# Three idle engines read elements of x into registers at the start of an Lp-pooling kernel

## The chip, the cores and the metric

The kernel runs on one core of one Trainium2 chip. The metric is the device time of one execution in microseconds (us); the time given for a kernel is the median over several runs.

## What is computed

The input x is 32 x 256 x 4096 in float32, p is 2 and the window is 4. For each window of four neighbouring elements the kernel gives the root of the mean of the squares:

```python
for i in range(out_length):
    window = np.abs(x[:, :, 4 * i:4 * i + 4]) ** 2.0
    result[:, :, i] = np.mean(window, axis=-1) ** 0.5
```

The output is 32 x 256 x 1024 in float32. So 134.22 MB are read and 33.55 MB are written.

## The kernel before

**Tiling.** x is taken as one flat line of elements, since windows never cross a row. The line is cut into six blocks (`blocks`, line 51) of four, four, four, four, three and one tiles. Inside a block each of the 128 partitions holds one contiguous stretch (`rows`, line 64). A tile is 128 x 13184 elements (`W`, line 41), a few are narrower, and there are 20 of them. A row of a full tile, 52,736 bytes, is what one packet of a DMA moves; 128 rows over 16 DMA engines make eight packets on each engine. Neighbouring partitions of block 0 lie 52,704 elements apart in x, about 211 KB.

**Buffers.** x has three buffers (`x_tiles`, `X_SLOTS` is 3), so tile i uses buffer i mod 3. The results of a block of four tiles gather in `o_tile` (four places) until the block is stored; a sum that can't go there yet waits in PSUM (`s_tile`).

**Work on one tile.** ScalarE squares the tile in place (`square`, line 89). VectorE adds the first half of each window to the second (`pairs`, line 95), then the two sums that are left (`fours`, line 99). ScalarE takes the root (`root`, line 102). For the last two tiles VectorE squares a part itself (line 155).

**Order of the work.** It is written out by hand (`manual_schedule`): each engine runs its instructions in the order of the text. SyncE issues all loads (line 83): the first three at the very start (the loop over `X_SLOTS`, lines 122 and 123), load i+3 when VectorE is done with tile i. ScalarE issues the stores of the first three blocks from its own queue (line 86), SyncE those of the last three. The loads and SyncE's stores go by queue q1, ScalarE's stores by queue q10; both run on the same 16 DMA engines. TensorE has nothing to do in the kernel, GpSimd nothing but four small fills of constants before it. A barrier of all engines stands ahead of the kernel's first instruction (line 189 in the profile) and another after its last (line 203).

Of the kernel before, what the change touches and what calls it, by code (L numbers as in the profile page):

```python
# [1 line left out]

# [4 lines left out]


@with_exitstack
def kernel(  # L10
    ctx: ExitStack,
    tc: tile.TileContext,
    x: bass.AP,
    p: float,
    kernel_size: int,
    out: bass.AP,
):

    nc = tc.nc

    assert float(p) == 2.0, "kernel specialized for p == 2"
    k = int(kernel_size)  # L30
    assert k == 4, "kernel specialized for kernel_size == 4"

    P = nc.NUM_PARTITIONS
    fp32 = mybir.dt.float32
    Act = mybir.ActivationFunctionType
    add = mybir.AluOpType.add
    xf = x.rearrange("b c l -> (b c l)")
    of = out.rearrange("b c l -> (b c l)")
    total = xf.shape[0] // P

    W = 13184
    R = W // k
    X_SLOTS = 3
    NARROW = W - 32
    LAST = total - 18 * W - NARROW
    widths = [W] * 3 + [NARROW] + [W] * 15 + [LAST]
    n = len(widths)
    assert 0 < LAST <= W and LAST % 16 == 0


    blocks = [[0, 1, 2, 3], [4, 5, 6, 7], [8, 9, 10, 11], [12, 13, 14, 15], [18, 16, 17], [19]]
    block_of = {i: b for b, group in enumerate(blocks) for i in group}
    block_width = [sum(widths[i] for i in group) for group in blocks]

    x_pool = ctx.enter_context(tc.tile_pool(name="x_pool", bufs=1))
    o_pool = ctx.enter_context(tc.tile_pool(name="o_pool", bufs=1))
    s_pool = ctx.enter_context(tc.tile_pool(name="s_pool", bufs=1, space=bass.MemoryType.PSUM))
    x_tiles = [x_pool.tile([P, W], fp32, name=f"xt{j}") for j in range(X_SLOTS)]
    o_tile = o_pool.tile([P, 4 * R], fp32, name="ot")
    first = o_pool.tile([P, 1], fp32, name="first")  # L60
    s_tile = s_pool.tile([P, 4096], fp32, name="st")
    ctx.enter_context(tc.manual_schedule())

    def rows(flat, b, div):
        at = sum(block_width[:b]) * P // div
        return flat[at:at + block_width[b] * P // div].rearrange("(p w) -> p w", p=P)


    free = x_tiles[17 % X_SLOTS]
    place = {i: o_tile[:, i % 4 * R:i % 4 * R + widths[i] // k] for i in range(16)}  # L70
    place[18] = free[:, R:2 * R]
    place[19] = free[:, 0:LAST // k]
    place[16] = free[:, 2 * R:3 * R]
    place[17] = free[:, 3 * R:4 * R]
    held = [o_tile[:, 0:w // k] for w in block_width[:4]] + [free[:, R:4 * R], place[19]]

    xs, loads, stores, sums, squares = {}, {}, {}, {}, {}

    def load(i):
        b = block_of[i]  # L80
        at = sum(widths[j] for j in blocks[b][:blocks[b].index(i)])
        xs[i] = x_tiles[i % X_SLOTS][:, 0:widths[i]]
        loads[i] = nc.sync.dma_start(out=xs[i], in_=rows(xf, b, 1)[:, at:at + widths[i]])  # L83

    def store(b, queue):
        stores[b] = queue.dma_start(out=rows(of, b, k), in_=held[b])  # L86

    def square(v):
        return nc.scalar.activation(out=v, in_=v, func=Act.Square)  # L89

    def pairs(v):

        q = v.rearrange("p (n j) -> p n j", j=k)
        h = v[:, 0:v.shape[1] // 2].rearrange("p (n j) -> p n j", j=2)
        return nc.vector.tensor_tensor(out=h, in0=q[:, :, 0:2], in1=q[:, :, 2:4], op=add)  # L95

    def fours(o, v):
        h = v[:, 0:v.shape[1] // 2].rearrange("p (n j) -> p n j", j=2)
        return nc.vector.tensor_tensor(out=o, in0=h[:, :, 0], in1=h[:, :, 1], op=add)  # L99

    def root(o, s):
        return nc.scalar.activation(out=o, in_=s, func=Act.Sqrt, scale=1.0 / k)  # L102

    summed = {i: s_tile[:, 0:R] if i in (4, 8, 12, 16) else place[i] for i in range(n)}

    def roots(*group):
        if len(group) == 1:
            root(place[group[0]], summed[group[0]])
        else:
            v = o_tile[:, group[0] % 4 * R:(group[-1] % 4 + 1) * R]  # L110
            r = root(v, v)
            if group[0] in (5, 9):

                implied(r, stores[block_of[group[0]] - 1])
        if group[-1] in (3, 7, 11):
            store(block_of[group[-1]], nc.scalar)

    def implied(later, earlier):

        tc.declare_no_dep(later.ins, earlier.ins, reason="implied by the other waits")  # L120

    for i in range(X_SLOTS):
        load(i)


    ahead = {4: (3,), 8: (7,), 12: (11,)}
    behind = {3: [(0, 1, 2)], 7: [(5, 6), (4,)], 11: [(9, 10), (8,)], 14: [(12,)], 15: [(13, 14)], 16: [(15,)]}

    root(first[:, :], nc.const_aps.tensor(1.0, (P, 1), fp32))
    for i in range(17):  # L130
        if i in ahead:
            roots(*ahead[i])
        s = square(xs[i])
        squares[i] = s
        if i == 3:
            implied(s, squares[0])
        if i in (3, 7, 11):

            for earlier in sums[i - X_SLOTS]:
                implied(s, earlier)  # L140
        for group in behind.get(i, []):
            roots(*group)
        sums[i] = pairs(xs[i]), fours(summed[i], xs[i])
        if i + X_SLOTS < n:
            load(i + X_SLOTS)

    store(3, nc.sync)
    square(xs[17])
    pairs(xs[17])
    fours(summed[17], xs[17])  # L150
    later = {18: 4608, 19: 2000}

    def shared_square(i):
        v = xs[i][:, 0:later[i]]
        nc.vector.tensor_tensor(out=v, in0=v, in1=v, op=mybir.AluOpType.mult)  # L155
        square(xs[i][:, later[i]:widths[i]])

    def shared_pairs(i):
        implied(pairs(xs[i]), loads[i])

    shared_square(18)
    roots(16)
    roots(17)
    shared_pairs(18)
    fours(summed[18], xs[18])
    shared_square(19)
    roots(18)
    store(4, nc.sync)
    shared_pairs(19)
    fours(summed[19], xs[19])  # L170
    roots(19)
    store(5, nc.sync)


# [1 line left out]
_INS = ['x', 'p', 'kernel_size']  # L176
_OUTS = [((32, 256, 1024), 'float32')]

_NUMBERS = {'p': 2.0, 'kernel_size': 4}


# [26 lines left out]
```

## Time and profile before

| | |
|---|---|
| median of 3 runs | 393.96 us (393.93 to 393.99) |
| span of the profiled execution, first instruction to last | 392.3 us |
| what lies around the span: median less span | 1.7 us |
| HBM read, written | 134.22 MB, 33.55 MB |
| mean rate over the span | 428 GB/s |
| busy: ScalarE (ACT), VectorE (DVE), GpSimd (POOL) | 274.4 us, 218.2 us, 0.2 us |

The profile gives no time of the profiled execution but its span. In the profile's lines SP is SyncE, and a q behind an engine's name (SPq, ACTq, DVEq) stands for its instruction queue: issues and waits, not work. A view of windows cuts the span into stretches that one names; its columns are the stretch, its length, the busy time and the number of instructions of DVE, ACT and POOL, the granted TensorE clock, the DMA share and the rate. It books a DMA packet whole in the stretch in which it starts. So the rate times the length is the size of the packets that started there, and the DMA share times the length times 16, over their number, is how long one of them took.

### The profile page before, as it was taken

The numbers are of one execution on the slowest core, as the hardware profiler recorded it, in microseconds if no ns is written. First come the engines' busy times: TensorE is split into PE (matmuls) and PEld (weight loads), VectorE is DVE, ScalarE is ACT, GpSimd is POOL, SyncE is SP. The second block draws the span as 40 slices with busy tenths as digits, with TensorE's granted clock in tenths as the row PEclk, the third lists the DMA queues.
The fourth block names the chain that finished last, engine by engine and source line by source line (L and its number), as shares of the span: only waits on it lengthen the run. The fifth ranks groups of instructions, "written<-read, shape, count | busy, mean of one in ns | idle before, by whom it ended". The sixth has DMA issues, their size and how long they took to land.

```text
span 392.3 us, 176 instructions
## 1 busy us (share of the span) xinstructions
DVE 218.2 (56%) x42; ACT 274.4 (70%) x37; POOL 0.2 (0%) x4
## 2 busy tenths in 40 slices
DVE  0009477580693274905942748069418485699970
ACT  1095695979950859799509597995098999969910
POOL 0000000000000000000000000000000000000000
DMA  8999999999999999999999999999999999999997
GB/s 344 430 430 430 430 440 435 452 457 366 430 430 430 430 430 430 430 441 446 452 446 441 436 430 436 430 430 430 430 430 430 430 430 430 430 453 415 430 413 342
DMA packets 3744, 167.77 MB, mean 428 GB/s; under 512 B 416, under 2 KB 416, under 8 KB 416
## 3 DMA queue, kind: packets, MB, share of 16 engines
q1 hardware_dynamic: 3312, 147.53, 87.4%
q10 hardware_dynamic: 432, 20.25, 11.9%
HBM read 134.22 MB, written 33.55 MB: 428 GB/s over the span
## 4 chain that ended last, share of the span: by engine, by line
DMA 43%; ACT 30%; DVE 23%; issue 0%; ACTq 0%; SPq 0%; DVEq 0%
DMA xt<-in_x_dram 43%; ACT xt L89 28%; DVE xt L95 14%; DVE ot L99 5%; DVE xt L99 3%; DVE xt L155 2%; ACT ot L102 2%; ACT xt L102 1%; ACTq L86 0%; SPq L83 0%; DVEq L95 0%
## 5 line engine op out<-in xcount | busy, mean ns | idle before, releaser
L89 ACT ACTIVATE xt<-xt 128x13184 f32<-128x13184 f32 (+3 forms) x20 | 216.7, 10847 | 92.3 <-DMA xt<-in_x_dram 91.0
L95 DVE TENSOR_TENSOR xt<-xt 128x6592 f32<-128x6592 f32 (+2 forms) x20 | 139.7, 6985 | 144.1 <-ACT xt L89 143.9
L99 DVE TENSOR_TENSOR ot<-xt 128x3296 f32<-128x3296 f32 (+1 forms) x13 | 46.7, 3592 | 17.9 <-DMA out_dram<-ot 17.6
L102 ACT ACTIVATE ot<-ot 128x6592 f32<-128x6592 f32 (+3 forms) x8 | 37.2, 4655 | 7.0 <-DVE ot L99 7.0
L102 ACT ACTIVATE xt<-xt 128x3296 f32<-128x3296 f32 (+1 forms) x3 | 8.5, 2836 | 8.8 <-DVE xt L99 8.8
L99 DVE TENSOR_TENSOR st<-xt 128x3296 f32<-128x3296 f32 x4 | 14.4, 3600 | 0.1
L99 DVE TENSOR_TENSOR xt<-xt 128x3296 f32<-128x3296 f32 (+1 forms) x3 | 10.4, 3461 | 0.1
L102 ACT ACTIVATE ot<-st 128x3296 f32<-128x3296 f32 x3 | 8.7, 2898 | 0.0
L155 DVE TENSOR_TENSOR xt<-xt 128x4608 f32<-128x4608 f32 (+1 forms) x2 | 7.2, 3593 | 0.0
L102 ACT ACTIVATE xt<-st 128x3296 f32<-128x3296 f32 x1 | 2.9, 2898 | 0.0
L102 ACT ACT_TABLE_LOAD x1 | 1.3, 1283 | 0.7 <-PEq L189 0.7
L102 ACT ACTIVATE first<-const-float32-1.0 128x1 f32<-128x1 f32 x1 | 0.2, 202 | 0.0
L189 POOL MEMSET const-bfloat16-1.0<- 128x1 bf16 x1 | 0.1, 101 | 0.0
L189 POOL MEMSET const-uint8-127<- 128x1 uint8 x1 | 0.1, 101 | 0.0
L189 POOL MEMSET const-float32-0.0<- 128x1 f32 x1 | 0.1, 98 | 0.2 <-issue 0.2
L189 POOL MEMSET const-float32-1.0<- 128x1 f32 x1 | 0.1, 98 | 0.0
## 6 DMA issues: line engine op xcount, KB each, us to landing
xt<-in_x_dram SPq DMA_DIRECT2D x18, 6592.0 KB, 29.8
out_dram<-ot ACTq DMA_DIRECT2D x2, 6592.0 KB, 35.1
out_dram<-ot SPq DMA_DIRECT2D x1, 6592.0 KB, 37.1
out_dram<-ot ACTq DMA_DIRECT2D x1, 6588.0 KB, 36.3
xt<-in_x_dram SPq DMA_DIRECT2D x1, 6576.0 KB, 24.7
xt<-in_x_dram SPq DMA_DIRECT2D x1, 5840.0 KB, 21.9
out_dram<-xt SPq DMA_DIRECT2D x1, 4944.0 KB, 16.1
out_dram<-xt SPq DMA_DIRECT2D x1, 1460.0 KB, 8.2
```

Source lines behind the costliest of these rows:

```text
L89: return nc.scalar.activation(out=v, in_=v, func=Act.Square)
L95: return nc.vector.tensor_tensor(out=h, in0=q[:, :, 0:2], in1=q[:, :, 2:4], op=add)
L99: return nc.vector.tensor_tensor(out=o, in0=h[:, :, 0], in1=h[:, :, 1], op=add)
L102: return nc.scalar.activation(out=o, in_=s, func=Act.Sqrt, scale=1.0 / k)
L155: nc.vector.tensor_tensor(out=v, in0=v, in1=v, op=mybir.AluOpType.mult)
L189: nc = _bacc.Bacc("TRN2", target_bir_lowering=False, num_devices=1)
```

## The change

Ahead of the first three loads, in the text, four reads are added by a loop: each takes the first 32 bits of one partition's stretch of block 0 into a register of an engine. TensorE reads those of partitions 0 and 1, GpSimd that of partition 64, VectorE that of partition 127. Nothing uses the values. No other line is changed.

```diff
+    ints = rows(xf, 0, 1).bitcast(mybir.dt.int32)
+    for engine, p in ((nc.tensor, 0), (nc.tensor, 1), (nc.gpsimd, P // 2), (nc.vector, P - 1)):
+        seen = engine.alloc_register(f"seen{p}")
+        engine.load(seen, ints[p:p + 1, 0:1])
+        engine.keepalive_nop([engine.lower_val_access(seen)])
     for i in range(X_SLOTS):
         load(i)
```

Built, each read of an element is two register loads, one of the address of x (named `in_x_dram_ptr` in the built program) and, after a sum on the register, one of the element. TensorE's program grows from one row, a branch, to seven, with four register loads; GpSimd's and VectorE's get three rows each, two of them register loads. On VectorE they stand ahead of its first addition, on GpSimd behind the four fills and the barrier. The programs of ScalarE and SyncE have the same rows and the same waits as before.

## The prediction

> **What bounds the kernel now.** I read the page first: how busy each engine is, and how full the DMA is.
>
> ```profile
> DVE 218.2 (56%) x42; ACT 274.4 (70%) x37; POOL 0.2 (0%) x4
> ...
> DMA  8999999999999999999999999999999999999997
> ...
> q1 hardware_dynamic: 3312, 147.53, 87.4%
> q10 hardware_dynamic: 432, 20.25, 11.9%
> ```
>
> No engine is full, but the two DMA queues together hold the 16 DMA engines for 87.4% + 11.9% = 99.3% of the span. Only the first and the last slice fall short of nines. The kernel is bound by its transfers, and what can still be won lies at the two ends, or where a packet takes longer than its bytes need.
>
> Next the chain of work that ended last (start, length, what), its first pieces and its last:
>
> ```profile
> 0.66 0.07 issue
> 0.73 18.04 DMA xt<-in_x_dram
> 18.77 0.02 issue
> 18.79 11.20 ACT xt L89
> 29.99 0.02 issue
> 30.01 7.04 DVE xt L95
> ...
> 306.43 24.79 DMA xt<-in_x_dram
> 331.22 0.02 issue
> 331.25 11.20 ACT xt L89
> ...
> 380.49 0.02 issue
> 380.51 2.64 ACT xt L102
> ```
>
> The chain begins with SyncE's first issue at 0.73 and the landing of tile 0 at 18.77. From the landing at 331.22 on it is compute up to 383.15, then the last store. In between, transfers and compute hand over to each other many times, yet the DMA is never out of work: load 3 is issued at 40.75 while load 2 lands only at 49.9. So **the whole program hangs rigidly on the landing of tile 0**: every later issue follows a landing, and every landing follows the packets before it. A microsecond won or lost before 18.77 should be there at the end too, one for one. No row shows a slack that would swallow it.
>
> Last, the windows at the start, and around the first packets of the first and the second store (91.8 and 172.5):
>
> ```profile
> 1.70:2.30 0.60, 0.00 (x0) 0.51 (x2) 0.00 (x0) 1.00 4.24 1318
> 2.30:2.60 0.30, 0.00 (x0) 0.00 (x0) 0.00 (x0) 1.00 0.42 176
> 2.60:4.30 1.70, 0.00 (x0) 0.00 (x0) 0.00 (x0) 1.00 0.00 0
> 4.30:4.85 0.55, 0.00 (x0) 0.00 (x0) 0.00 (x0) 1.00 3.55 1534
> 91.80:92.40 0.60, 0.00 (x0) 0.60 (x1) 0.00 (x0) 1.00 4.82 1406
> 172.50:173.30 0.80, 0.00 (x0) 0.80 (x1) 0.00 (x0) 1.00 2.43 1055
> ```
>
> In the first two, 1318 GB/s x 0.60 us is 15 packets and 176 x 0.30 is one: the first packet of each of the 16 DMA engines. They took (4.24 x 0.60 + 0.42 x 0.30) x 16 / 16 = 2.67 us each. The second packets, from 4.30 on, took 3.55 x 0.55 = 1.95 us, and that stays the pace. So **the first packet costs 0.72 us too much on average**, and no engine starts another before 4.34. By the packet records the first ones start from 1.74 to 2.49 and last 2.01 to 3.00 us, the second ones start from 4.34 to 4.80. Taking 1.95 off, each engine is as if it had begun between 2.39 and 2.85.
>
> The same happens once more. In the window at 91.80, 16 load packets took 4.82 x 0.60 = 2.89 us, 0.94 too much, just as the first store comes on (ScalarE issued it at 90.31). At the second store they took 2.43 x 0.80 = 1.95: nothing.
>
> **The change part by part.** It removes and moves nothing, and adds no wait: the rows of SyncE and ScalarE stay as they are, so no DMA is moved past another.
>
> *The instructions themselves.* TensorE's four register loads, and two each on GpSimd and VectorE, start after the barrier, at about 0.75 us. VectorE's first addition starts at 30.01, because ScalarE's first square ends only then; TensorE and GpSimd have nothing before the barrier at the end, past 391 us. The trace has no register load. The nearest rows are a semaphore instruction on a queue, 0.02 us, from below, and SyncE's issue to its first packet, 0.73 to 1.74, so 1.0 us, from above. Two in a row on VectorE are 0.04 to 2.0 us, beside 29 us of cover; TensorE's four at most 4.0. I take **nothing**. Were the cover gone, VectorE's 2 us would delay the issue of load 3, which has 9 us (40.75 to 49.9) before the queue runs dry.
>
> *What the reads do to the first packets.* This is the only place on the path. Suppose the excess of 0.72 us is paid by whoever first reaches x, and that the three engines' reads can pay it. The element's read leaves after the address is in, at 0.75 plus 0.02 to 1.0, so at 0.77 to 1.75; the DMA's first packet starts at 1.74. The head start is 0 to 0.97 us, the middle 0.48. What it is worth is set by the DMA engine that is last, not by the mean: the last is as if begun at 2.85, and if all excess went, the last would be the one that starts at 2.49 and has hardly any (2.01 against 1.95). So the gain is 2.85 - 2.49 = **0.36 us**; a head start of 0.36 is enough for it, and the middle one gives that. The ends: nothing, and 1.06, if the late starts were part of the excess too and all engines began at about 1.79. Below nothing: reads that stand in front of the DMA's own could cost as much as they can win, 0.36.
>
> [...] No row of before shows a register load.
>
> *Sum.* The profiled execution's 392.3 would become 391.9. The 1.7 us around the span don't change, as no row of them is touched, so the median of 393.96 goes to **393.6**.
>
> **The rivals.**
>
> *The excess isn't about x (393.96).* The window at 91.80 speaks for this: 0.94 us are lost when a second queue starts, on load packets that read x, which had been read for 90 us. At that time no store packet had begun. If the excess is a queue's own start, q1 has one at 1.74 and q10 one at 91.8, and a read from another engine takes away neither. Against it: the first packets of q1 were under way when they lost the time, and `out` is first used at 91.8 as well, so a first touch of a tensor fits both places too; tiles of later blocks, 27 MB on, show no excess.
>
> [...]
>
> *The reads come too late (393.96).* They do what they say, but if a register load takes the full 1.0 us, the element's read leaves at 1.75, with the DMA's own.
>
> *The reads take away more (392.9 to 393.3).* If the staggered starts, 1.74 to 2.49, belong to the excess, the last engine begins at 2.2 (the later spread is 4.34 to 4.80, 0.46) or at 1.79: 0.65 to 1.06 us are won. For it: the last of the 16 starts alone, 0.28 after the one before. Against it: the stagger is mostly what the 0.38 us of SyncE's issue would make.
>
> *Slower (395.0).* If first reaches to x are served one after the other, and two of the three engines' reads go out before 1.74, to stretches of x far apart (partitions 0 and 64, 13.5 MB), the DMA waits for both: 2 x 0.72 us, less the 0.36 that is then paid for it, is 1.08 more. It decides only where the reads are early and take turns. Against it: 16 DMA engines reach 16 places of x at once and lose 0.72 on average, not 16 times that.
>
> **How the numbers follow.** Forecast, 393.6: 0.42. More won: 0.15. Not about x: 0.26. Too late: 0.09. Slower: 0.08. The range, 392.9 to 394.3, takes in the bound of 1.06 and the 0.36 below nothing, and leaves out the slower case and a little. A measurement of this kernel tells about 0.2% (0.79 us) from no change. Over 0.79 won is most of the second case and a little of the first, together 0.15; slower by as much is the last case, 0.08; all else, 0.77, is within.
>
> **What would show it.** Right: the windows from 1.70 to 2.60 give packets of about 2.2 us, tile 0 lands at about 18.4, and the end comes 0.36 earlier. If the packets still take 2.67, the rivals without effect hold. If the first packets start later than 1.74, or take over 2.67, the slower one. The 0.94 at 91.8 should stay. A gain ahead of 18.77 that is not there at the end would refute the rigid chain. If VectorE's first addition starts later than its square's end, the cover was wrong.

## The result, and the profile after

The changed kernel takes **394.45 us** (median of 20 runs, 394.17 to 395.11); the kernel before, beside it, 394.01 us (20 runs, 393.88 to 394.24). The ratio is 1.0012, with a 95% interval of 1.0006 to 1.0017: slower by 0.44 us, a tenth of a percent, and clear of zero. The forecast was 393.6 and its range ended at 394.3.

The page of the profiled execution of the changed kernel, against the lines shown of before:

```profile
span 392.0 us, 187 instructions
...
DVE 218.2 (56%) x42; ACT 274.4 (70%) x37; POOL 0.2 (0%) x4
...
DMA  8999999999999999999999999999999999999998
...
q1 hardware_dynamic: 3312, 147.53, 87.4%
q10 hardware_dynamic: 432, 20.25, 11.9%
```

The work and the transfers are the same. The span is even a little shorter, 392.0 against 392.3. But this very execution took 394.17 us, so **2.2 us lie around the span, where 1.7 to 1.8 lay before**. Each run lists its span beside its time. Over the 20 runs of the changed kernel the span is 392.28 us on average and the rest 2.20 us; over the 33 runs of before that the first experiments were measured beside, 392.26 and 1.78. All of the 0.44 us, but for 0.02, stands where the profile shows nothing.

The windows at the start, of the changed kernel:

```profile
1.70:2.30 0.60, 0.00 (x0) 0.52 (x2) 0.00 (x0) 1.00 4.58 1406
2.30:2.60 0.30, 0.00 (x0) 0.00 (x0) 0.00 (x0) 1.00 0.00 0
2.60:4.30 1.70, 0.00 (x0) 0.00 (x0) 0.00 (x0) 1.00 0.00 0
4.30:4.85 0.55, 0.00 (x0) 0.00 (x0) 0.00 (x0) 1.00 3.56 1534
91.80:92.40 0.60, 0.00 (x0) 0.60 (x1) 0.00 (x0) 1.00 4.54 1406
```

The 16 first packets take 4.58 x 0.60 = 2.75 us each, before 2.67: the reads have taken nothing away. Nor is the 0.08 more a loss: over the profiled executions of all 20 kernels of this document that mean goes from 2.62 to 2.76. The next view, of the added line alone, shows why they could not. Its columns are the operation, how often, the shortest, median and longest duration in ns, and the first and last start in us; PEldq is TensorE's queue.

```profile
L125 PEldq TENSOR_LOAD <-in_x_dram_ptr x2: 1221/2444/3667, 0.8 to 5.0; - x2
L125 PEldq TENSOR_LOAD <-in_x_dram x2: 2201/2518/2835, 2.1 to 8.8; - x2
L125 POOLq TENSOR_LOAD <-in_x_dram_ptr x1: 1181/1181/1181, 0.7 to 0.7; - x1
L125 DVEq TENSOR_LOAD <-in_x_dram_ptr x1: 1143/1143/1143, 0.8 to 0.8; - x1
...
L125 POOLq TENSOR_LOAD <-in_x_dram x1: 2894/2894/2894, 2.0 to 2.0; - x1
L125 DVEq TENSOR_LOAD <-in_x_dram x1: 2784/2784/2784, 2.0 to 2.0; - x1
```

Fetching the first address takes 1.14 to 1.22 us, so the first element is asked for at 2.0, when the DMA engines have been reading x since 1.75. The first element of each engine then takes 2.8 to 2.9 us, beside the full DMA. TensorE is done at 11 us, VectorE at 4.8, well ahead of its first addition at 30.06.

Two questions are left. Where do the 0.42 us around the span come from? And would an earlier read have helped?

### The profile page after: what moved, and what is told of

Read it like the earlier page. It is cut to its first block, busy times and chain, and to the rows that moved or that the text cites. A ratio compares the mean times of both kernels' runs of the same rounds, so it can differ in the third digit from the quotient of the medians.

```text
span 392.0 us, 187 instructions
## 1 busy us (share of the span) xinstructions
DVE 218.2 (56%) x42; ACT 274.4 (70%) x37; POOL 0.2 (0%) x4
## 4 chain that ended last, share of the span: by engine, by line
DMA 43%; ACT 31%; DVE 23%; issue 0%; ACTq 0%; SPq 0%; DVEq 0%
DMA xt<-in_x_dram 43%; ACT xt L89 28%; DVE xt L95 14%; DVE ot L99 5%; DVE xt L99 3%; DVE xt L160 2%; ACT ot L102 2%; ACT xt L102 1%; ACTq L86 0%; SPq L83 0%; DVEq L95 0%
```

## The experiments

"Around" below is the time of a run less its span, averaged over the runs of a kernel (5 to 33 of them, each to 0.1 us in the span). The records of VectorE are all that its queue shows in the span: work, waits, drains and register instructions.

| kernel | VectorE's records | around, us | mean span, us | median, us |
|---|---|---|---|---|
| before (33 runs) | 53 | 1.78 | 392.26 | 393.99 |
| changed (20 runs) | 56 | 2.20 | 392.28 | 394.45 |
| TensorE's reads alone | 53 | 1.78 | 392.23 | 393.96 |
| GpSimd's read alone | 53 | 1.78 | 392.32 | 394.05 |
| VectorE's read alone | 56 | 2.21 | 392.27 | 394.52 |
| reads of SBUF in place of x | 54 | 2.05 | 392.26 | 394.33 |
| 3 fills on VectorE | 56 | 2.20 | 392.27 | 394.43 |
| 3 reads of SBUF on VectorE | 56 | 2.21 | 392.23 | 394.47 |
| VectorE's read at the end | 56 | 2.21 | 392.27 | 394.45 |
| two squares off VectorE | 49 | 1.77 | 393.86 | 395.66 |
| the same, with VectorE's read | 52 | 1.79 | 394.08 | 395.88 |
| 1 fill on VectorE | 54 | 2.05 | 392.21 | 394.25 |
| 12 fills on VectorE | 65 | 1.78 | 392.63 | 394.39 |
| 16 fills on VectorE | 69 | 1.79 | 392.65 | 394.45 |
| 64 fills on VectorE | 117 | 1.78 | 392.48 | 394.17 |
| changed, and 61 fills on VectorE | 117 | 1.75 | 392.53 | 394.18 |

Four more kernels, with VectorE's 53 records as before, follow further down; their time around the span is 1.77 to 1.79 us.

### Which engine's reads cost

Three kernels keep the reads of one engine each (TensorE's shown); a fourth keeps all four but reads a constant in SBUF.

```diff
-    for engine, p in ((nc.tensor, 0), (nc.tensor, 1), (nc.gpsimd, P // 2), (nc.vector, P - 1)):
+    for engine, p in ((nc.tensor, 0), (nc.tensor, 1)):
```

```diff
-    ints = rows(xf, 0, 1).bitcast(mybir.dt.int32)
+    ints = nc.const_aps.tensor(1.0, (P, 1), fp32).bitcast(mybir.dt.int32)
```

Expected, TensorE alone:

> TensorE's two reads alone; GpSimd and VectorE read nothing. With all reads the device time rose from 394.01 to 394.45 us while the profiled span fell from 392.26 to 391.98, so the time around the span went from 1.7 to 2.2 us. Theory 1 (an engine that otherwise does nothing, or reaches no HBM tensor, costs time around the span as soon as its program holds such reads): the time around the span is over 1.7 us, by the whole 0.5 us if TensorE carries it, by some 0.2 us if the engines share it; the span stays within 0.3 us of 392.26. Theory 2 (the reads disturb the DMA inside the span): time around the span stays 1.7 us and the span itself grows in most runs. Theory 3 (the two kernels only differ by how they were drawn): no difference beyond 0.1 us.

GpSimd alone:

> GpSimd's read alone. Theory 1: the time around the span is over 1.7 us, by 0.5 us if GpSimd carries it, by some 0.2 us if the engines share it. Theory 2: around the span 1.7 us, and the span differs. Theory 3: no difference beyond 0.1 us.

VectorE alone:

> VectorE's read alone. Theory 1: the time around the span is over 1.7 us, by 0.5 us if VectorE carries it, by some 0.2 us if the engines share it. Theory 2: around the span 1.7 us, and the span differs. Theory 3: no difference beyond 0.1 us.

SBUF in place of x:

> The same four reads on the same three engines, but of a constant in SBUF (one register load each, no address to fetch) in place of x in HBM. Theory 1 in the form that what counts is reaching an HBM tensor: 394.0 us, 1.7 us around the span. Theory 1 in the form that what counts is any register load in an engine's program: 394.45, 2.2 us around the span. Theory 2: the span as before, since HBM isn't touched. The first packets of the DMA take 2.67 us each as before, as nothing of x is read ahead.

Measured: 1.78, 1.78, 2.21 and 2.05 us around the span. **VectorE's read carries the whole cost**, and the spans are alike, which refutes theories 2 and 3. Theory 1 falls too in both its forms: TensorE, which had done nothing before, reads x at no cost, and reads that never leave the chip cost 0.27 us. The SBUF kernel has one record more on VectorE, the read of x makes three more. So the next theories are about a register load on VectorE (A) and about any instruction more on it (B).

### A register load, or any instruction

`spare` in these diffs is a small tile that the edit adds for the purpose.

```diff
+    for j in range(3):
+        nc.vector.memset(spare[:, j:j + 1], 1.0)
     for i in range(X_SLOTS):
```

Expected, three fills and no read at all:

> Three fills of one column of a spare tile ahead of VectorE's first addition, no register and no read: three instructions more in VectorE's program, as many as its read of x makes. So far the time around the span was 1.78 us before, 1.78 with TensorE's or GpSimd's reads, 2.05 with one register load from SBUF on VectorE, 2.21 with VectorE's read of x. Theory A (a register load in VectorE's program is what costs): 1.78 us around the span, 394.0 in all. Theory B (any instruction more in VectorE's program costs, some 0.14 to 0.27 us each): 2.2 us or more around the span, 394.4 or more in all. The span stays 392.2 to 392.3 in both.

Three reads of SBUF by VectorE alone:

> VectorE alone reads three constants from SBUF into registers. Theory A, as a charge for having any: 2.05 us around the span, as with one. Theory A by the load, or theory B by the instruction: 0.27 us each, 2.6 us, or, if the second and third count less as between one load (2.05) and address, sum and element (2.21), some 2.2 us. The span stays 392.2 to 392.3.

VectorE's read of x behind its last addition:

```diff
     fours(summed[19], xs[19])
...
+    seen = nc.vector.alloc_register("seen")
+    nc.vector.load(seen, ints[P - 1:P, 0:1])
...
```

> VectorE's read of x stands behind its last addition, at about 380.5 us, beside ScalarE's last root and the last store, in place of the start. If the cost hangs on the reads being there (theories A and B): 2.2 us around the span, 394.5 in all. If it hangs on their being the first instructions or on the DMA's start: 1.78 us, 394.0.

Two squares less on VectorE, in `shared_square`:

```diff
-        v = xs[i][:, 0:later[i]]
-        nc.vector.tensor_tensor(out=v, in0=v, in1=v, op=mybir.AluOpType.mult)
-        square(xs[i][:, later[i]:widths[i]])
+        square(xs[i])
```

> ScalarE squares the last two tiles whole, so VectorE has two squares and their waits less; the rest as before. The span grows, as the last tiles wait longer for ScalarE; only the time around the span is asked for. Theory B (the length of VectorE's program): below 1.78 us, by 0.14 to 0.27 us for each instruction less, 1.2 to 1.5 us. Theory A: 1.78 us.

Measured: 2.20, 2.21, 2.21 and 1.77 us. Three fills, without a register or a read, cost the same 0.42 us as the read of x, and the read costs it at the far end of the program too. **Theory A falls; it is neither the read nor its place but three instructions more.** Theory B as it stood falls as well: four records less bring nothing. There is an edge, and the kernel before stands just on its free side.

### Where the edge is

One fill (the edit is shown against the kernel with three) and, in the same way, 64; and VectorE's read of x, at the start, added to the kernel with two squares less, so that the program is no longer than before:

```diff
-    for j in range(3):
+    for j in range(1):
         nc.vector.memset(spare[:, j:j + 1], 1.0)
```

```diff
+    seen = nc.vector.alloc_register("seen")
+    nc.vector.load(seen, ints[P - 1:P, 0:1])
...
     for i in range(X_SLOTS):
...
-        nc.vector.tensor_tensor(out=v, in0=v, in1=v, op=mybir.AluOpType.mult)
...
+        square(xs[i])
```

> One fill on VectorE in place of three (which gave 2.20 us around the span, before 1.78, two squares less 1.77). Theory B1 (the length of VectorE's program counts from an edge that the program before just reaches): as with the one register load from SBUF, 2.05 us around the span, 394.3 in all. A step that one instruction already takes whole: 2.2 us, 394.45. If it counts what the instruction is: 1.78.

> 64 fills on VectorE, some 6 us of work ahead of its first addition at 30.0 us, so hidden. If each instruction past the edge costs, as from one (0.27) to three (0.42): 0.07 us for each more, some 6 us around the span. If it is a step that three instructions have taken whole: 2.2 us. If the program's place in blocks that are fetched counts, it may be back at 1.78. The span stays 392.2 to 392.3.

> VectorE reads x as in the change, but ScalarE squares the last two tiles whole, so VectorE's program is no longer than before (four records less, three more). The span is that of the kernel with two squares less, 393.9. Length theory: 1.78 us around the span although the read is there, 395.65 in all. If the read itself counted: 2.2 us, 396.1.

Measured: 2.05, 1.78 and 1.79 us. One fill costs what one SBUF read did. The read in a program of 52 records is free around the span. And 64 fills are free around it too: past the edge it does not go on rising, it goes away. Inside the span of that kernel, though, the timeline (start, length, engine, line, operation, idle time before it) shows something new:

```profile
0.80 1.75 DVE L124 MEMSET spare<- 128x1 f32 x61 [0.80 <-PEq L192]
2.02 0.20 ACT L103 ACTIVATE first<-const-float32-1.0 128x1 f32<-128x1 f32 x1
2.93 0.12 DVE L124 MEMSET spare<- 128x1 f32 x3 [0.38 <-issue]
```

After 61 fills, 0.03 us apart, VectorE stands still for 0.38 us and waits for nothing that the profile shows; with the 0.03 us that neighbours overlap it is a step of 0.41. It comes ahead of VectorE's 64th record in the span: two records of the opening barrier and 61 fills stand before it. A second thing is new: in the table of queues of this kernel's DMA there is a third one, with one packet of 8,192 bytes that started at 8.27 and took 0.31 us, in the window from 8 to 9:

```profile
q1 hardware_dynamic: 16, 0.84, 198.2%
q14 instruction: 1, 0.01, 1.9%
```

The tables of the kernels before and after, which cover the span, have no such line.

The next two runs ask whether the reads change anything in this (the changed kernel with 61 fills), and what happens between 3 and 64 (16 fills, no reads).

```diff
         engine.load(seen, ints[p:p + 1, 0:1])
         engine.keepalive_nop([engine.lower_val_access(seen)])
+    for j in range(61):
+        nc.vector.memset(spare[:, j:j + 1], 1.0)
```

> The changed kernel whole, with 61 fills more on VectorE behind its read, so that its program is 64 instructions longer than before, as in the run with 64 fills, which had 1.78 us around the span. If the length alone counts: 1.78 us around the span, 394.0 to 394.2 in all, with all four reads in place. If the reads have a charge of their own: 2.2 us.

> 16 fills on VectorE. One gave 2.05 us around the span, three 2.20, 64 gave 1.78. If the charge holds until some block is full: 2.2 us or more. If it goes with the place within a short stretch of instructions: 1.78.

Measured: 1.75 and 1.79 us. **With all four reads in place the charge around the span is gone** once the program is 64 longer, as with fills alone; the step of 0.41 us stands again ahead of the 64th record (two of the barrier, three of the read and 58 fills come before it; the read holds VectorE until 4.7), and the packet of instructions follows at 10.2. The mean span is 0.27 us longer than before, which neither the step nor the read explains.

```profile
4.75 1.67 DVE L129 MEMSET spare<- 128x1 f32 x58 [4.75 <-issue]
6.79 0.12 DVE L129 MEMSET spare<- 128x1 f32 x3 [0.38 <-issue]
```

With 16 fills the total is back at 394.45, but now the span has it: 392.65. The timeline of VectorE at the end of that kernel:

```profile
365.10 3.59 DVE L100 TENSOR_TENSOR xt<-xt 128x3296 f32<-128x3296 f32 x1
368.61 2.23 DVE L158 TENSOR_TENSOR xt<-xt 128x2000 f32<-128x2000 f32 x1
371.36 6.24 DVE L96 TENSOR_TENSOR xt<-xt 128x5840 f32<-128x5840 f32 x1 [0.52 <-DVE xt L158]
377.64 3.20 DVE L100 TENSOR_TENSOR xt<-xt 128x2920 f32<-128x2920 f32 x1
```

And of the kernel before:

```profile
365.16 3.59 DVE L99 TENSOR_TENSOR xt<-xt 128x3296 f32<-128x3296 f32 x1
368.67 2.23 DVE L155 TENSOR_TENSOR xt<-xt 128x2000 f32<-128x2000 f32 x1
371.00 6.24 DVE L95 TENSOR_TENSOR xt<-xt 128x5840 f32<-128x5840 f32 x1
377.28 3.20 DVE L99 TENSOR_TENSOR xt<-xt 128x2920 f32<-128x2920 f32 x1
```

From 368.61 to 371.36 there are 2.75 us, before from 368.67 to 371.00 2.33: 0.42 us, on the chain that ends last. The addition that starts late is VectorE's 64th record. The view names the square before it as the releaser, but that one is done at 370.84. So the same step, at the same place in VectorE's program, is paid where that place falls: hidden ahead of the first addition with 64 fills, on the chain with 16.

A last run, with 12 fills in place of 16, puts it into the span's closing barrier.

```diff
-    for j in range(16):
+    for j in range(12):
```

> 12 fills on VectorE: its program has 65 recorded instructions in the span, and the step ahead of the 64th falls among its last ones, the closing barrier at 391.6. If that step is what is paid behind the span with one and three fills: the time around the span is 1.78 us again, the span is longer by up to 0.4 us, and a gap of some 0.4 us stands among VectorE's records in the closing barrier; the total is 394.2 to 394.5. If the charge behind the span has another cause: around the span 2.05 to 2.2 us as with one and three.

Measured: 1.78 us around, a span of 392.63, 394.39 in all. The closing records of this kernel, then of before (the last number ahead of the dash is the start of the last one):

```profile
L206 DVEq DRAIN x2: 143/1688/3233, 377.4 to 392.4; - x2
L206 ACTq DRAIN x2: 14/1340/2666, 380.6 to 391.9; - x2
```

```profile
L203 DVEq DRAIN x2: 19/1627/3235, 377.3 to 391.9; - x2
L203 ACTq DRAIN x2: 14/1339/2664, 380.5 to 391.8; - x2
```

VectorE's last drain starts 0.5 us behind ScalarE's, before at nearly the same time. It is its 64th record again, 0.50 us after the wait ahead of it where 0.09 stood before, 0.41 more.

So **VectorE loses 0.41 to 0.42 us ahead of its 64th record, be it a fill, an addition or a drain**, in the four kernels with 65 records or more. In the kernel before, the span ends with its 53rd record. That the 0.27 and 0.42 us around the span are the same step, met behind it by what VectorE runs there when the program is one or three instructions longer, is the reading that fits all 16 rows of the table. It is argued and not shown: no trace has VectorE's records behind the span, the time around it isn't split into what lies ahead and what lies behind, and no kernel here has 57 to 64 records. Why one instruction costs 0.27 and three 0.42 stays open.

That the step is VectorE's alone isn't shown either. With their reads TensorE has 11 records and GpSimd 19, so these two runs, with 1.78 us around the span, say only that their longer programs cost nothing, far from a 64th record. SyncE has 56 in two of the runs that follow, as many as VectorE in the changed kernel, and the time around the span is 1.78 in both.

A queue of instructions, q14 in the table above, and a packet of 8,192 bytes on it are in all four traces. Whether the 0.41 us have to do with that packet isn't shown. In all four traces the packet starts after the step (at 8.27 after 2.93, 10.20 after 6.79, 375.35 after 371.36, and with 12 fills at 393.06 after 392.37, there already behind the span), so VectorE doesn't wait for that packet in the step; what it waits for isn't shown. The traces with 54 and 56 records hold no such packet from the start of the span on; ahead of it the trace of before has six, the first 10.98 us and the last 8.18 us before the span, and that of the changed kernel five, from 11.22 to 8.27.

### Would an earlier read have paid for the first packets

SyncE reads the first element of x itself and only then issues the loads.

```diff
+    seen = nc.sync.alloc_register("seen")
+    nc.sync.load(seen, ints[0:1, 0:1])
...
     for i in range(X_SLOTS):
```

> SyncE itself reads the first element of x and issues the first load only when it has it, so everything starts later by the two register loads, 0.9 + 0.9 to 2.8 us by the rows of the other engines. Asked for are the first packets. If their excess of 0.72 us is a first reach to x that a read can pay: they take 1.95 us each, and some of the delay comes back. If it belongs to the queue or to the DMA's start: 2.67 us as before. Around the span: 1.78, as VectorE's program is unchanged.

Its reads, and the windows of the first packets (16 of them from 3.20 on):

```profile
L124 SPq TENSOR_LOAD <-in_x_dram_ptr x1: 847/847/847, 0.7 to 0.7; - x1
L124 SPq TENSOR_LOAD <-in_x_dram x1: 647/647/647, 1.6 to 1.6; - x1
```

```profile
3.20:4.10 0.90, 0.00 (x0) 0.00 (x0) 0.00 (x0) 1.00 3.02 938
```

The element is there at 2.24, a microsecond ahead of the first packet, and the packets still take 3.02 x 0.90 = 2.72 us. **A read of x by an engine doesn't pay for the first packets**, at least not the read of partition 0's element. Four traces above say the same for a read that goes out with the DMA: with TensorE's, GpSimd's or VectorE's reads alone, and with 61 fills behind all four, the first address takes 0.90 to 0.93 us, the elements are asked for at 1.70 to 1.81, the DMA's first packet starts at 1.74 to 1.76, and the first packets take 2.64 to 2.69. The run shows the rigid chain too: SyncE's first issue is 1.55 us later (2.28 after 0.73), and the mean span 1.56 us longer (393.82 after 392.26).

### What the 0.94 us at 91.8 belong to

Three kernels, each with one edit to the kernel before: ScalarE starts q10 early, with a load of one element of x for each partition; SyncE writes two elements of each partition's stretch of `out` early, behind the first three loads (the real store writes them again; GpSimd fills the two elements beforehand); SyncE issues the first store on q1 in place of ScalarE on q10.

```diff
+    nc.scalar.dma_start(out=spare[:, :], in_=rows(xf, 0, 1)[:, 0:1])
     root(first[:, :], nc.const_aps.tensor(1.0, (P, 1), fp32))
```

```diff
+    nc.sync.dma_start(out=rows(of, 0, k)[:, 0:2], in_=spare[:, :])
     root(first[:, :], nc.const_aps.tensor(1.0, (P, 1), fp32))
```

```diff
-            store(block_of[group[-1]], nc.scalar)
+            store(block_of[group[-1]], nc.sync if group[-1] == 3 else nc.scalar)
```

> ScalarE starts its queue q10 at the beginning, with a load of one element per partition of x into a spare tile; its first store comes later as before. If the 0.94 us lost at 91.8 is the start of a queue: it is gone there (load packets at 91.8 take 1.95 us, not 2.89), paid at the start where the DMA has to begin anyway, and the span falls by up to 0.9 us. If it is the first reach to out: 2.8 to 2.9 us at 91.8 as before, and the span is 392.2 to 392.4.

> SyncE writes two elements of each partition's stretch of out on queue q1, behind the first three loads, so out is first reached at some 50 us; the real store of these elements follows at 91.8 on q10. If the excess at 91.8 is the first reach to out: it goes to some 50 us or vanishes, and the packets at 91.8 take 1.95 us. If it is the start of q10: they take 2.8 to 2.9 us as before. The extra instructions are SyncE's and GpSimd's, so the time around the span stays 1.78 us.

> The first store goes out by SyncE on q1 in place of ScalarE on q10, at the same point (some 90.3 us); the second, at about 169, is then q10's first. If the 0.94 us at 91.8 belong to the first store, whichever queue: load packets at 91.8 still take about 2.9 us and those at 172.5 take 1.95. If they belong to the first store on q10: 1.95 us at 91.8 and about 2.9 at 171 to 173. VectorE's program is as before: 1.78 us around the span.

Summed over the large packets from 86 to 99 us and divided by 16 engines, the time over the usual 1.947 us a packet is 1.00 us before, 0.84 with q10 started early, 0.94 with `out` reached early. In the other kernels, whose edits don't touch it, it goes from 0.83 to 1.07, so neither edit takes anything away that can be told. With the first store on q1 it is 0.02 there, and 0.85 between 100 and 113. The windows of that kernel:

```profile
91.80:92.40 0.60, 0.00 (x0) 0.60 (x1) 0.00 (x0) 1.00 3.25 1406
107.30:108.30 1.00, 1.00 (x1) 1.00 (x1) 0.00 (x0) 1.00 2.20 844
109.30:110.30 1.00, 1.00 (x1) 1.00 (x1) 0.00 (x0) 1.00 2.54 844
172.20:173.20 1.00, 0.00 (x0) 1.00 (x1) 0.00 (x0) 1.00 2.07 844
```

At 91.80 the 16 packets take 3.25 x 0.60 = 1.95 us. Those from 107.3 and 109.3 on take 2.20 and 2.54, and at the first store on q10, from 172.2 on, they take 2.07. So most of the loss **follows the program's first large store, whichever queue it is on**, and neither the queue's start nor a first small write to `out`. A part may stay with the queue: from 165 to 185 us the same sum is 0.15 here and 0.00 to 0.01 in every other kernel. What in a first large store costs it stays open, and so does the cause of the 0.72 us of the first packets. None of the three is faster than the kernel before: 394.09, 394.27 and 394.61 us.

## Why the prediction was wrong

- **The step that failed: "The 1.7 us around the span don't change, as no row of them is touched."** They changed by 0.42 us, all of the result but for 0.02. The three rows more on VectorE were priced by what they do, at most 2 us beside 29 us of cover. They took 4.0, and the cover held: by that account they cost nothing. What was missed is that they make VectorE's program longer: three fills cost the same 0.42 us, and in a program longer still the charge around the span is gone with all reads in place. That it is the step ahead of the 64th record, pushed to where it is paid, is the reading argued above. Neither the forecast nor a rival held this term; the rival for slower put its mechanism at the memory, ahead of the first packets, and the mean span stayed, 392.28 against 392.26.
- **The gain of 0.36 us was nothing.** It rested on a head start of 0 to 0.97 us. Both of its conditions fail. The address takes 1.14 to 1.22 us in the profiled execution, over the bound of 1.0 taken from SyncE's issue to its first packet, so the reads came 0.25 us after the DMA: the rival "too late". In four other kernels it took 0.90 to 0.93, and the head start was then 0.06 us at most. And when the read is early, in the SyncE run, it pays for nothing, as the rival "not about x" had it; whether the excess has to do with x all the same stays open. Both rivals gave 393.96 and had 0.35 of the chance; for the span they were right, 392.28 against 392.26.
- *The instructions themselves at nothing* held: VectorE's first addition starts at 30.06, 0.03 us after its square ends. But the bounds of the duration did not, 2.0 us for VectorE and 4.0 for TensorE: VectorE's reads take 4.0 and TensorE's end at 11 us, with one load of 3.67. The nearest row, SyncE's issue to its first packet, was from a time when no load was under way, and these loads ran beside the DMA's.
- The bounds of one register load, 0.02 and 1.0 us, held in the SyncE run: 0.85 us for the address and 0.65 for the element, both read while no load was under way. Beside the running loads an element took 2.0 to 3.0 us.
- *The whole program hangs rigidly on the landing of tile 0* held: 1.55 us of delay at the start came out as 1.56 at the end. The 0.42 us of the run with 16 fills came out at the end as 0.39 (392.65 less 392.26).
- Of the causes weighed for the 0.94 at 91.8, the start of a second queue fell as the main one: 0.85 us follow the first large store to q1, and 0.15 at most stay with q10. A first touch of `out` got no support, as an early write to every partition's stretch left it in place; whether other bytes of those stretches count was not tried.

## What to carry to other kernels

Three instructions that cost nothing where they stood still made this kernel 0.42 us longer, fills and reads alike: they made VectorE's program longer. Price the length of the program as well as the work, and try it by adding instructions that do nothing of use. When the spans of two kernels agree and their times don't, compare time less span over many runs; one profile of each would have called this change a gain of 0.3 us. And take the bound of an operation that the trace lacks from a time when as much is under way as will be: here it came from a time without loads and was 1.0 us, and the element's reads took 2.0 to 3.0 us beside the loads.

## What the runs showed that was not expected

- In the four kernels with 65 records or more VectorE stood still for 0.41 to 0.42 us ahead of its 64th record in the span, be it a fill, an addition or a drain; a packet of instructions, 8,192 bytes in 0.31 to 0.46 us, followed 0.7 to 5.3 us later. With 64 fills, where VectorE's own step is hidden, the mean span is still 0.22 us longer than before; why isn't shown.
- In these kernels a register load of x or of its address took 0.65 to 1.2 us ahead of the first packets and 2.0 to 4.2 us beside the running loads; beside a store alone, at the end of the program, 0.74 to 0.93. A load of a constant in SBUF took 0.31 to 0.55.
- The first large store of this program costs a DMA engine 0.83 to 1.07 us on average, once; put on the other queue, it still costs 0.85.
